# A conditioned block and two layers on one core: products of p @ w_ple moved to the ends of three projections, sums of squares added on VectorE

## The chip, the core and the metric

One core of one Trainium2 chip runs the whole program. The time is device microseconds of one execution. The engines are TensorE (PE; its weight loads are PEld), VectorE (DVE), ScalarE (ACT), GpSimd (POOL, nearly unused here) and SyncE (SP), which issues the loads. A line such as L357 is a line of the kernel.

## What is computed

256 tokens of width 2048 go through a block with conditioning (first_block) and two layers. What matters here:

```
# end of first_block's mixer, and what follows
x = x + gt_a * merge_heads(att_l, conv_l, g_mix_out, w_out)      # mix @ w_out
hf_l = modulate(rms_norm(x, g_ffn_norm), sh_f, sc_f)
x = x + gt_f * conv_ffn(hf_l, w_up, ffn_conv_w, ffn_conv_b, w_down)
x = rms_norm(x, g_final)
# the two layers i = 0, 1 (mixers A and B)
    h = mixer(x, ..., w_o)                      # (o * silu(gate)) @ w_o
    x = layer_norm(ALPHA * x + h, ln_g[i], ln_b[i])
    x = x + (p[i] @ w_ple[i]) * sigmoid(x @ w_ple_gate[i])
```

p[i] is an input of 256 x 256 and w_ple[i] is 256 x 2048, so p @ w_ple depends on nothing that the program computes.

## The kernel before

Activations lie with the features on the 128 partitions: X is [128, 16 tiles, 256 tokens]. Everything is float32, and each product is made of three: the weight is split into a high part wh (a cast on ScalarE, L357) and a low part wl (a subtraction on VectorE, L358), the activation into XH and XL in the same way, and TensorE adds wh·XH, wl·XH and wh·XL (L409). A unit is a piece of weights of 128x1024, 24 products of 256 columns.

The weights come from memory as raw chunks of 1 MB, two units each, through one queue on SyncE (L338), in a fixed order that plan() writes down. There are four raw buffers and five of split weights. unit() first splits up to four units ahead (look), unless hold() says that they must wait: units of w_up and w_pg are split ahead only for the first three, (0,0), (0,2) and (1,0) (group, first k tile). Between the units of the first block, chunks of w_ada ("late" events, L347, 128x2048 each) are summed on VectorE in the same order.

A projection of 2048 columns is computed in groups of 512 or 256 columns (_specs). MR and SR hand out accumulators in PSUM; a group's first product waits until the accumulator's last reader is done. Work that follows a group (gen) is written as generators that pump() takes a step further after each unit; this fixes every engine's order when the program is built. Each engine then runs its instructions strictly in that order.

resid(...) is a projection that ends in a residual sum: after each group upd adds its tiles to X; squares (sqr, on ScalarE) are added up in acc on VectorE; the last group's squares go one by one through a product with a matrix of ones (sums), which gives the sum over all features (s). It serves w_out (of the first block, groups 512, 512, 512, 256, 256), w_down, and the output projections woA and woB of the two layers (four groups of 512).

At the end of w_out, rstd makes the norm's factor RF, hf_first() the first two tiles of XH and XL for w_up, and hf(1) the next two. The layers' finish_layer issues the load of p (PF, "pf"), runs resid for the output projection with fin(0) converting PF to PH and PL, then the first group of w_ple, the sums, the second group, the norm's steps (gen_ln), the third and fourth groups, and then w_pg, whose first pairs of tiles are normed by pair(q). keep copies the ple products from PSUM to PW.

In the views in_wout, in_wada, in_woA, in_pt and so on are the inputs in memory, s and m accumulators in PSUM, rsm and RF the norm's numbers in the first block, mu, var and rsl those of a layer, and ADA the sums over w_ada.

Of the kernel before, what the change touches and what calls it, by code (L numbers as in the profile page):

```python
# [78 lines left out]
def _specs():  # L79
# [16 lines left out]
        "woA": (KD, [512] * 4),  # L96
# [6 lines left out]
        "woB": (KD, [512] * 4),  # L103
# [5 lines left out]
def _layout(kt, groups):  # L109

    chunks, cur, off = [], [], 0
    for g, w in enumerate(groups):
        uk = 1024 // w
        for k0 in range(0, kt, uk):
            nk = min(uk, kt - k0)
            if off + nk * w > 2048 or (kt > 2 and cur and cur[0][0] != g):
# [96 lines left out]
def _body(st, tc, A, out, dbg):  # L213
# [3 lines left out]
    lay = {n: _layout(*s) for n, s in spec.items()}  # L217
# [64 lines left out]
    plan_with_late("wout", [0, 4, 1, 5, 2, 6, 3, 7] + list(range(8, 16)))  # L282
    three = [4 * g + c for c in range(4) for g in range(3)]
    plan_with_late("wup", three + list(range(12, len(lay["wup"]))))
    for n in ("wdown", "wiq", "wik", "wka", "wva", "wqA", "wgA", "woA", "wple0", "wpg0", "wkb", "wvb", "wqB",
              "wgB", "woB", "wple1", "wpg1"):
        c = list(range(len(lay[n])))
        plan(n, three + c[12:] if n in ("wpg0", "wpg1") else c)
# [5 lines left out]
    pp = st.enter_context(tc.tile_pool(name="pp", bufs=1, space=PSUM))  # L294

# [120 lines left out]
    def unit_b(name, g, pst, xh, xl, starts=(0, 2)):  # L416

        u = unit(name, g)
# [102 lines left out]
    ones = cp.tile([P, P], F32, name="ones")  # L521
    identb = cp.tile([P, P], BF16, name="identb")
# [22 lines left out]
    def newton(dst, m):  # L545

        S.activation(dst, m, AF.Ln)
# [20 lines left out]
    with tc.tile_pool(name="b0", bufs=1) as b0:  # L568
# [29 lines left out]
        V.memset(ones, 1.0)  # L598

# [408 lines left out]
    def resid(pool, name, xh_, xl_, upd, acc, fin=None, pre=None, first=(), into=None):  # L1008
# [3 lines left out]
        n_acc = acc.shape[1]  # L1012
        tot = []

        def gen(g, m):
# [22 lines left out]
            if g == 2:  # L1038
                V.tensor_tensor(acc[:, :, 0], acc[:, :, 0], acc[:, :, 1], OP.add)
                for _ in range(3):  # L1040
                    yield
                b = yield from SR.get()
                mm(b.t[:, :n_acc * T], ones, acc[:, :, 0], True, False)
                tot.append(b)
# [4 lines left out]
        sq = pool.tile([P, 4, T], F32, name="sqe", tag="sqe")  # L1049

# [6 lines left out]
        def sums(ns):  # L1057
            for n in ns:
                if n_acc == 2:
                    mm(tot[0].t[:, T:], ones, X[:, n, :], False, n == 15)  # L1060
                mm(tot[0].t[:, :T], ones, sq[:, n - 12], False, n == 15)

        def gen_end(m, ns):
            yield
            end(m, ns)
            while not tot:
                yield
            for _ in range(3):
                yield
            sums(ns)  # L1070

        halves = len(spec[name][1]) == 5
        if halves:
            EV.add(gen_end(group_b(name, 3, xh_, xl_), (12, 13)))
            pump()
            end(group_b(name, 4, xh_, xl_), (14, 15))
        else:
            end(group_b(name, 3, xh_, xl_), range(12, 16))
# [5 lines left out]
        if fin:  # L1084
            fin(3)

# [4 lines left out]
        def finish():  # L1091
# [3 lines left out]
            sums((14, 15) if halves else range(12, 16))  # L1095
# [40 lines left out]
    with tc.tile_pool(name="b2", bufs=1) as b2:  # L1136
# [9 lines left out]
        b = resid(b2, "wout", xh, xl, upd_out, acc, first=m_out)()  # L1146
        rstd(RF, b.t[:, :T], 1.0 / D, EPS)
# [43 lines left out]
        hf_first()  # L1191
        for _ in hf(1):
            pass

        AC = b2.tile([P, NF, T], F32, name="AC")

# [58 lines left out]
        fin2 = resid(b2, "wdown", lambda k, u: u.x[:, 0, k - u.k0], lambda k, u: u.x[:, 1, k - u.k0], upd_down, acc, fin_lo, fin_hi, into=RF)  # L1255
        dump("x2", X)

        def gen_rf():
# [4 lines left out]
            yield from rstd_steps(RF, tot2.t[:, :T], 1.0 / D, EPS)  # L1263
# [69 lines left out]
    def finish_layer(pool, layer, wo, wp, wg, last):  # L1333

        PF = pool.tile([P, 2, T], F32, name="pf")
        nc.sync.dma_start(PF, A["pt"][layer])
        PH = pool.tile([P, 2, T], F32R, name="ph")
        PL = pool.tile([P, 2, T], F32R, name="pl")
        acc = pool.tile([P, 2, 2, T], F32, name="accl")
        PW = pool.tile([P, KD, T], F32, name="PW")  # L1340

# [3 lines left out]
        def fin(g):  # L1345
            if g == 0:
                pin()
                S.copy(PH, PF)
                V.tensor_tensor(PL, PF, PH.bitcast(F32), OP.subtract)

        finish = resid(pool, wo, xh, xl, upd, acc, fin)
# [4 lines left out]
        def gen_ln(tot):  # L1356
            ps = tot.t
            V.tensor_scalar(mu, ps[:, T:], 1.0 / D, None, op0=OP.mult)
            V.tensor_tensor(v, mu, mu, OP.mult)
            V.scalar_tensor_tensor(v, ps[:, :T], 1.0 / D, v, op0=OP.mult, op1=OP.subtract)  # L1360
            tot.free()
            V.tensor_scalar(v, v, 0.0, LN_EPS, op0=OP.max, op1=OP.add)
            yield from newton(rs, v)
            V.tensor_tensor(mu, mu, rs, OP.mult)
            both(pair(0), pair(1))
# [13 lines left out]
        def ple(g):  # L1379
            return group_b(wp, g, lambda k, u: PH[:, k, :], lambda k, u: PL[:, k, :])  # L1380

        def keep(g, m):
            S.copy(PW[:, 4 * g:4 * g + 4, :], four(m.t))
            m.free()

        m0 = ple(0)
        ln = gen_ln(finish())
        m1 = ple(1)
        keep(0, m0)
        next(ln)  # L1390
# [521 lines left out]
```

## Time and profile before

| | |
|---|---|
| three runs | 2202.58, 2196.92, 2197.62 us (median 2197.62) |
| profiled execution | 2194.55 us, span 2192.7 us |
| mean granted clock of TensorE | 0.993 |
| busy share of the span | TensorE 98%, VectorE 68%, ScalarE 50% |
| moved by DMA | 467.71 MB, mean 213 GB/s |
| chain that ended last | TensorE 94%, DMA 2%, VectorE 2%, ScalarE 1% |

The busy share says how long an engine had an instruction in hand. The chain is followed back from the last instruction, at each step to what released it. A row of a timeline has in brackets how long the engine stood idle before the instruction and which instruction ended that.

### The profile page before, as it was taken

How to read it: one execution, taken by the hardware profiler on the slowest of the kernel's cores; microseconds unless marked ns; L12 is line 12 of the kernel's file. 1: busy time of each engine (PE TensorE's matmuls, PEld its weight loads, DVE VectorE, ACT ScalarE, POOL GpSimd, SP SyncE). 2: the span in 40 equal slices, each digit the busy share in tenths (PEclk: the TensorE clock that was granted, in tenths of full speed). 3: DMA queues.
4: the chain of work that ended last, by engine and by line, in shares of the span. 5: the costliest groups of instructions: out<-in, count | busy, mean ns of one | idle time of the engine just before them, and what ended most of it. 6: DMA issues, size and time to landing. Idle time of an engine off the chain costs nothing.

```text
span 2192.7 us, 40082 instructions
## 1 busy us (share of the span) xinstructions
PE 2148.4 (98%) x17272; PEld 2058.8 (94%) x17272; DVE 1494.7 (68%) x1992; ACT 1104.9 (50%) x1512; POOL 0.2 (0%) x4
## 2 busy tenths in 40 slices
PE   5999999999999999999999999999999999999999
PEld 3779789989999999999999999999999999999999
DVE  4457878878767676757877669666666746646575
ACT  4345455445544444445656443445446546645363
POOL 0000000000000000000000000000000000000000
PEclk9999999999999999999999999999999999999999
DMA  9874878867666666645555544444555554455553
GB/s 395 335 278 175 324 260 308 344 242 288 230 223 239 231 233 236 223 176 190 187 187 187 186 164 177 150 154 154 197 174 181 188 192 142 147 173 190 181 176 113
DMA packets 68434, 467.71 MB, mean 213 GB/s; under 512 B 7840, under 2 KB 8352, under 8 KB 16544
## 3 DMA queue, kind: packets, MB, share of 16 engines
q1 hardware_dynamic: 68256, 465.14, 58.6%
q8 instruction: 135, 2.21, 0.4%
q14 instruction: 43, 0.35, 0.0%
HBM read 463.01 MB, written 2.10 MB: 212 GB/s over the span
## 4 chain that ended last, share of the span: by engine, by line
PE 94%; DMA 2%; DVE 2%; ACT 1%; issue 0%; SPq 0%; DVEq 0%; ACTq 0%
PE m L409 80%; PE s L409 14%; DMA raw<-in_wada 1%; DMA rawx<-in_wqa 1%; PE s L406 1%; DVE wl L358 1%; ACT wh L357 0%; DMA X<-in_xt 0%; DVE sq L616 0%; DVE raw L347 0%; DVE rp L1285 0%; DVE rp L1286 0%; DVE X L1144 0%; ACT uf L1204 0%; DVE uf L1212 0%
## 5 line engine op out<-in xcount | busy, mean ns | idle before, releaser
L409 PE MATMUL m<-XH,wh 128*128 128x256 f32 x4032 | 1144.8, 284 | 5.8 <-ACT XH L1185 4.1
L358 DVE TENSOR_TENSOR wl<-raw,wh 128x1024 fp32r<-128x1024 f32 (+1 forms) x672 | 800.2, 1197 | 502.9 <-ACT wh L357 501.6
L409 PE MATMUL m<-XH,wl 128*128 128x256 f32 x4032 | 1133.2, 281 | 2.9 <-DVE wl L358 2.9
L409 PE MATMUL m<-XL,wh 128*128 128x256 f32 x4032 | 1133.2, 281 | 0.3 <-DVE XL L1188 0.3
L357 ACT CAST wh<-raw 128x1024 fp32r<-128x1024 f32 (+1 forms) x672 | 687.0, 1029 | 665.8 <-PE m L409 587.4
L409 PEld LDWEIGHTS m<-XH,wh 128*128 128x128 f32 x4032 | 762.7, 189 | 27.6 <-issue 20.7
L409 PEld LDWEIGHTS m<-XH,wl 128*128 128x128 f32 x4032 | 762.5, 189 | 6.4 <-DVE wl L358 3.3
L409 PEld LDWEIGHTS m<-XL,wh 128*128 128x128 f32 x4032 | 762.2, 189 | 0.7 <-DVE XL L1188 0.6
L409 PE MATMUL m<-ahl,wh 128*128 128x256 f32 x1376 | 245.0, 281 | 0.5 <-DVE uf L1213 0.5
L409 PEld LDWEIGHTS m<-ahl,wh 128*128 128x128 f32 x1376 | 211.3, 188 | 0.7 <-issue 0.7
L409 PE MATMUL m<-ahl,wl 128*128 128x256 f32 x688 | 193.1, 281 | 0.0
L347 DVE SCALAR_TENSOR_TENSOR raw<-raw,CBC 128x2048 f32<-128x2048 f32 x64 | 145.0, 2283 | 0.0
L409 PEld LDWEIGHTS m<-ahl,wl 128*128 128x128 f32 x688 | 129.7, 189 | 0.0
L409 PE MATMUL s<-XH,wh 128*128 128x256 f32 x416 | 117.9, 283 | 7.1 <-ACT XH L649 7.1
L409 PE MATMUL s<-XL,wh 128*128 128x256 f32 x416 | 117.9, 283 | 0.0
L409 PE MATMUL s<-XH,wl 128*128 128x256 f32 x416 | 117.6, 283 | 0.0
L362 ACT CAST ahl<-AC 128x512 fp32r<-128x512 f32 x88 | 53.7, 610 | 89.0 <-PE m L409 89.0
L409 PEld LDWEIGHTS s<-XH,wh 128*128 128x128 f32 x416 | 79.4, 191 | 7.3 <-ACT XH L649 7.3
L363 DVE TENSOR_TENSOR ahl<-AC,ahl 128x512 fp32r<-128x512 f32 x88 | 59.6, 677 | 38.5 <-ACT ahl L362 38.5
L409 PEld LDWEIGHTS s<-XH,wl 128*128 128x128 f32 x416 | 79.4, 191 | 0.0
L409 PEld LDWEIGHTS s<-XL,wh 128*128 128x128 f32 x416 | 79.4, 191 | 0.0
L358 DVE TENSOR_TENSOR wl<-rawx,wh 128x768 fp32r<-128x768 f32 (+1 forms) x24 | 25.0, 1046 | 60.7 <-ACT wh L357 60.7
(387 smaller groups left out, 1683.4 us busy)
## 6 DMA issues: line engine op xcount, KB each, us to landing
raw<-in_wada SPq DMA_DIRECT2D x96, 1024.0 KB, 7.0
raw<-in_wup SPq DMA_DIRECT2D x86, 1024.0 KB, 4.9
raw<-in_wdown SPq DMA_DIRECT2D x40, 1024.0 KB, 4.8
raw<-in_wpg SPq DMA_DIRECT2D x32, 1024.0 KB, 4.9
raw<-in_wconv SPq DMA_DIRECT2D x28, 768.0 KB, 5.6
raw<-in_wout SPq DMA_DIRECT2D x16, 1024.0 KB, 6.4
raw<-in_wqA SPq DMA_DIRECT2D x16, 1024.0 KB, 4.8
raw<-in_wgA SPq DMA_DIRECT2D x16, 1024.0 KB, 4.8
```

Source lines behind the costliest of these rows:

```text
L347: V.scalar_tensor_tensor(r, r, 1.0, CBC, op0=OP.mult, op1=OP.mult, accum_out=ADA[:, b:b + 1])
L357: S.copy(e.wh[:, :n], r)
L358: V.tensor_tensor(e.wl[:, :n], r, e.wh[:, :n].bitcast(F32), OP.subtract)
L362: S.copy(e.x[:, 0, :e.nk], a)
L363: V.tensor_tensor(e.x[:, 1, :e.nk], a, e.x[:, 0, :e.nk].bitcast(F32), OP.subtract)
L406: count[0] = TE.transpose(o, i, ident)
L409: count[0] = TE.matmul(ps, l, r, start=start, stop=stop, skip_group_check=True, **kw)
```

## The change

It has five parts.

- The groups of p @ w_ple are computed elsewhere: layer 0's groups 0 and 1 at the end of w_out; layer 0's groups 2 and 3 and layer 1's group 0 at the end of woA; layer 1's groups 1 to 3 at the end of woB. The first of the three goes between a projection's last product and its sums. What a later layer needs is copied from PSUM by ScalarE (keep), stored in memory (plek) by a DMA that ScalarE issues, and loaded again by SyncE.
- p is loaded by parts(), which issues the DMA, the conversion on ScalarE and the subtraction on VectorE one after another, ahead of the projection's groups: in w_out for layer 0, in woA for layers 0 and 1 (both through one buffer pf), in woB for layer 1.
- woA and woB get groups of 512, 512, 512, 256, 256. In resid, squares and values of tiles 12 and 13 are added on VectorE; only the last two tiles go through ones on their own.
- ones holds 1/2048 from w_out on, so the sums are means; Ln reads PSUM directly (rstd_mean).
- The first two tiles of a layer's norm are handled one by one (first_pair), and w_pg's accumulators are handed out in another order.

```diff
-        "woA": (KD, [512] * 4),            # the same for woB
+        "woA": (KD, [512] * 3 + [256] * 2),
...
     plan_with_late("wout", [0, 4, 1, 5, 2, 6, 3, 7] + list(range(8, 16)))
+    plan("wple0", [0])
...
+        plan(n, three + c[12:] if n in ("wpg0", "wpg1") else c[1:] if n in ("wple0", "wple1") else c)
+        if n == "wple0":
+            plan("wple1", [0])
...
+    def rstd_mean(dst, src):
+        m = cp.tile([P, T], F32, name="rsm", tag="rsm")
+        S.activation(dst, src, AF.Ln, bias=eps[:, 0:1])
+        V.tensor_scalar(m, src, EPS, None, op0=OP.add)
+        yield from newton(dst, m, False)
...
+    def ple(layer, g, ph, ahead):
+        m = Banks(SR.now(), SR.now()) if ple_at[0] == 0 else MR.now()
+        ple_at[0] += 1
+        unit_b(f"wple{layer}", g, lambda n: m.bank(n // 2)[:, n % 2 * T:(n % 2 + 1) * T],
+               lambda k, u: ph[:, 0, k, :], lambda k, u: ph[:, 1, k, :], ahead=ahead)
+        return m
+
+    def keep(dst, m):
+        for b in range(2):
+            S.copy(dst[:, 2 * b:2 * b + 2, :], m.bank(b).rearrange("p (b t) -> p b t", b=2))
+        m.free()
+
+    def parts(pool, layer, tags):
+        pf = pool.tile([P, 2, T], F32, name="pf", tag=tags[0], bufs=tags[1])
+        ph = pool.tile([P, 2, 2, T], F32R, name="ph", tag=tags[2], bufs=tags[3])
+        nc.sync.dma_start(pf, A["pt"][layer])
+        S.copy(ph[:, 0], pf)
+        V.tensor_tensor(ph[:, 1], pf, ph[:, 0].bitcast(F32), OP.subtract)
+        return ph
...
+        def gen_end(m):                    # in resid: tiles 12 and 13
+            yield
+            end(m, (12, 13))
+            yield
+            V.tensor_tensor(acc[:, 0], acc[:, 0], sq[:, 0:2], OP.add)
+            if n_acc == 2:
+                V.tensor_tensor(acc[:, 1], acc[:, 1], X[:, 12:14, :], OP.add)
+            fold()
+            for _ in range(2):
+                yield
+            yield from total()
...
+        if fill:
+            fill()
...
-            sums((14, 15) if halves else range(12, 16))
+            if n_acc == 2:
+                mm(b.t[:, T:], ones, sq[:, 0], False, True)
+            for n in (14, 15):
+                mm(b.t[:, :T], ones, sq[:, n - 12], False, n == 15)
...
-        b = resid(b2, "wout", xh, xl, upd_out, acc, first=m_out)()
-        rstd(RF, b.t[:, :T], 1.0 / D, EPS)
+        V.memset(ones, 1.0 / D)
+        W4 = dict(tag="w4", bufs=4)
+        ph = parts(b2, 0, ("w4", 4, "w4", 4))
+        ple_out, ple_kept = [], dp.tile([P, 12, T], F32, name="plek")
+        def fill_out():
+            ple_at[0] = 0
+            ple_out.append(ple(0, 0, ph, 3))
+        b = resid(b2, "wout", xh, xl, upd_out, acc, first=m_out, fill=fill_out, sqe=W4)()
+        ple_out.append(ple(0, 1, ph, 2))
+        for _ in rstd_mean(RF, b.t[:, :T]):
+            pass
...
         hf_first()
-        for _ in hf(1):
-            pass
+        for g, m in enumerate(ple_out):
+            keep(AC[:, 4 * g:4 * g + 4, :], m)
+            nc.scalar.dma_start(ple_kept[:, 4 * g:4 * g + 4, :], AC[:, 4 * g:4 * g + 4, :])
+            if g == 0:
+                for _ in hf(1):
+                    pass
...
+        jobs = ((1, 1), (1, 2), (1, 3)) if last else ((0, 2), (0, 3), (1, 0))   # in finish_layer
+        ph = {}
+        for n in dict.fromkeys(l for l, _ in jobs):
+            ph[n] = parts(pool, n, ("pf", 1, f"ph{n}", 1))
+        if last:
+            nc.sync.dma_start(PW[:, 0:4, :], ple_kept[:, 8:12, :])
+        else:
+            nc.sync.dma_start(PW[:, 0:8, :], ple_kept[:, 0:8, :])
...
+        def fill(i=0):
+            n, g = jobs[i]
+            out_banks.append(ple(n, g, ph[n], 3 - i))
+        def store(i):
+            n, g = jobs[i]
+            if n == layer:
+                keep(PW[:, 4 * g:4 * g + 4, :], out_banks[i])
+            else:
+                t = pool.tile([P, 4, T], F32, name="pn")
+                keep(t, out_banks[i])
+                nc.scalar.dma_start(ple_kept[:, 8:12, :], t)
+        tot = resid(pool, wo, xh, xl, upd, acc, fin, fill=fill)()
+        fill(1)
+        fill(2)
+        # mu, var, rsl from tot on VectorE and ScalarE, store(0) and store(1) between
+        first_pair()
+        both(pair(1))
+        store(2)
```

VectorE around the third group of w_out. raw,ADA is a chunk of w_ada, wl a weight's low part, gta the gate's numbers, and X<-m,gta,X adds a group's four tiles to X and is the last reader of the group's accumulator. Before:

```order
L347 SCALAR_TENSOR_TENSOR raw,ADA<-raw,CBC 128x2048 x2
L358 TENSOR_TENSOR wl<-raw,wh 128x1024 x4
L1141 TENSOR_TENSOR gta<-ADA,vecs 128x16
L1144 SCALAR_TENSOR_TENSOR X<-m,gta,X 128x256 x4
L347 SCALAR_TENSOR_TENSOR raw,ADA<-raw,CBC 128x2048 x2
```

And after:

```order
L351 SCALAR_TENSOR_TENSOR raw,ADA<-raw,CBC 128x2048 x2
L362 TENSOR_TENSOR wl<-raw,wh 128x1024 x4
L1192 TENSOR_TENSOR gta<-ADA,vecs 128x16
L1197 MEMSET ones 128x128
L1041 TENSOR_TENSOR ph<-pf,ph 128x512
L1195 SCALAR_TENSOR_TENSOR X<-m,gta,X 128x256 x4
L351 SCALAR_TENSOR_TENSOR raw,ADA<-raw,CBC 128x2048 x2
```

The memset and the subtraction of p's parts now stand between gta and the four X operations.

ScalarE at the start of layer 0's output projection. GTA is the mixer's gate, XH<-OA the high part of the mixer's output. Before:

```order
L357 CAST wh<-raw 128x1024 x2
L1329 ACTIVATE GTA<-GTA 128x512
L563 CAST XH<-OA 128x512
L1329 ACTIVATE GTA<-GTA 128x512
L563 CAST XH<-OA 128x512
L357 CAST wh<-raw 128x1024 x10
L1027 ACTIVATE sqr<-X 128x512 x2
L357 CAST wh<-raw 128x1024
L555 ACT_TABLE_LOAD
L1348 CAST ph<-pf 128x512
```

And after:

```order
L361 CAST wh<-raw 128x1024 x2
L1396 ACTIVATE GTA<-GTA 128x512
L576 CAST XH<-OA 128x512
L1396 ACTIVATE GTA<-GTA 128x512
L576 CAST XH<-OA 128x512
L1040 CAST ph<-pf 128x512 x2
L361 CAST wh<-raw 128x1024 x10
L1077 ACTIVATE sqr<-X 128x512 x2
```

Two conversions of p, one for each layer, now stand ahead of the weight conversions that follow the mixer; before, one stood eleven weight conversions later.

ScalarE at the end of layer 0's output projection. sqe are the last squares, rsl and var the norm's numbers, PW and pn the ple products, wh the units of w_pg. Before:

```order
L1054 ACTIVATE sqe<-X 128x256 x4
L357 CAST wh<-raw 128x1024 x2
L1383 COPY PW<-m 128x1024
L547 ACTIVATE rsl<-var 128x256
L548 ACTIVATE rsl<-rsl 128x256
L1383 COPY PW<-m 128x1024
L1373 ACTIVATE X<-X,vecs 128x256 x2
L1375 CAST XH<-X 128x512
L1373 ACTIVATE X<-X,vecs 128x256 x2
L1375 CAST XH<-X 128x512
L357 CAST wh<-raw 128x1024
L1383 COPY PW<-m 128x1024 x2
```

And after:

```order
L361 CAST wh<-raw 128x1024 x3
L1100 ACTIVATE sqe<-X 128x256 x2
L560 ACTIVATE rsl<-var 128x256
L561 ACTIVATE rsl<-rsl 128x256
L1032 COPY PW<-s 128x512 x2
L1032 COPY PW<-m 128x512 x2
L1461 ACTIVATE XH<-X,vecs 128x256 x2
L1473 ACTIVATE X<-X,vecs 128x256 x2
L1475 CAST XH<-X 128x512
L1032 COPY pn<-m 128x512 x2
L1433 DMA plek<-pn 128x1024
L361 CAST wh<-raw 128x1024 x5
```

After the norm's numbers ScalarE now has four copies, the first two tiles, one pair, two copies and a DMA issue ahead of the next weight conversion.

## Rows read from the trace of the kernel before

**Rows 1.** The page: first the line of TensorE in the part on busy time (us, share of the span, instructions; the lines of the weight loads and of the other engines stand beside it), then the row of VectorE's sums over the chunks of w_ada among the costliest groups (busy us and mean ns of one, idle time before them).

```profile
PE 2148.4 (98%) x17272; PEld 2058.8 (94%) x17272; DVE 1494.7 (68%) x1992; ACT 1104.9 (50%) x1512; POOL 0.2 (0%) x4
...
L347 DVE SCALAR_TENSOR_TENSOR raw<-raw,CBC 128x2048 f32<-128x2048 f32 x64 | 145.0, 2283 | 0.0
```

**Rows 2.** The view by windows, core 0: start and end in us, length, then busy us and instructions of PE, PEld, DVE, ACT and POOL, the granted clock, the DMA engines' mean share and GB/s. The third group of w_out, the end of w_out (two rows), and a stretch inside w_up.

```profile
435.50:437.20 1.70, 0.25 (x3) 0.07 (x2) 1.70 (x5) 0.00 (x0) 0.00 (x0) 1.00 1.02 434
...
485.50:489.90 4.40, 0.30 (x3) 0.26 (x2) 2.96 (x10) 1.75 (x4) 0.00 (x0) 1.00 0.00 0
...
489.90:493.30 3.40, 3.08 (x14) 2.71 (x14) 1.91 (x5) 1.53 (x4) 0.00 (x0) 0.50 0.00 0
...
600.00:700.00 100.00, 100.00 (x854) 100.00 (x853) 68.45 (x81) 47.76 (x60) 0.00 (x0) 1.00 0.65 232
```

**Rows 3.** The chain that ended last, in order of time, at the third group of w_out: start us, us, what.

```profile
435.40 1.67 DVE X L1144 x4
...
437.21 2.85 PE m L409 x22
```

**Rows 4.** The timeline of SyncE, which issues the loads: start us, us, queue, line, transfer, count. Four places.

```profile
121.62 1.02 SPq L509 DMA_DIRECT2D cst<-in_cst  x2
...
435.31 0.33 SPq L338 DMA_DIRECT2D raw<-in_wout  x1
...
1545.88 0.33 SPq L1336 DMA_DIRECT2D pf<-in_pt  x1
...
1996.46 0.33 SPq L1336 DMA_DIRECT2D pf<-in_pt  x1
```

**Rows 5.** DMA issues by window (transfer, queue, count, KB, us from issue to landing): the chunk issued at 435.31, the wada chunk issued between 121.1 and 121.3, the transfer of constants issued at 121.62, and pf issued at 1545.88 and at 1996.46.

```profile
raw<-in_wout SPq DMA_DIRECT2D x1, 1024.0 KB, 6.6
...
raw<-in_wada SPq DMA_DIRECT2D x1, 1024.0 KB, 15.0
...
cst<-in_cst SPq DMA_DIRECT2D x1, 256.0 KB, 15.2
...
pf<-in_pt SPq DMA_DIRECT2D x1, 256.0 KB, 3.5
...
pf<-in_pt SPq DMA_DIRECT2D x1, 256.0 KB, 2.9
```

**Rows 6.** The instructions on tile pf (ns min/median/max, first and last start in us, form).

```profile
L1348 ACT CAST ph<-pf x2: 622/623/624, 1570.9 to 2021.6; 128x512 fp32r<-128x512 f32 x2
...
L1349 DVE TENSOR_TENSOR pl<-pf,ph x2: 686/686/687, 1572.7 to 2023.3; 128x512 fp32r<-128x512 f32 x2
```

**Rows 7.** The chain again, at the end of w_out.

```profile
485.57 0.44 DVE rsm L541
```

**Rows 8.** The timeline of TensorE at the end of w_out: start us, us, engine, line, operation, count, and in brackets the idle time before it and what ended it. The first row is the sums that follow w_out's last product, the second the first product of w_up.

```profile
483.22 1.02 PE L409 MATMUL s<-sqe,ones 128*128 128x256 f32 x4
...
489.64 0.38 PE L409 MATMUL m<-XH,wh 128*128 128x256 f32 x1 [4.10 <-ACT XH L1185]
```

**Rows 9.** The timelines of VectorE and ScalarE, as above: the second XL tile of w_up's first unit, the activations of hf(1), and a copy of 128x512 out of PSUM.

```profile
490.85 0.43 DVE L1188 TENSOR_TENSOR XL<-th,XH 128x256 fp32r<-128x256 f32 x1
...
491.92 1.09 ACT L1169 ACTIVATE th<-th,shf,G 128x256 f32<-128x256 f32 x2 [1.84 <-DVE th L1165]
...
1510.54 0.58 ACT L1511 COPY pa<-s 128x512 f32<-128x512 f32 x1
```

**Rows 10.** The timelines of ScalarE, VectorE and TensorE at the start of layer 0's output projection, and ScalarE at that of layer 1 (third row).

```profile
1545.04 2.94 ACT L357 CAST wh<-raw 128x1024 fp32r<-128x1024 f32 x3
...
1551.66 1.05 ACT L357 CAST wh<-raw 128x1024 fp32r<-128x1024 f32 x1 [1.76 <-PE m L409]
...
2002.06 1.05 ACT L357 CAST wh<-raw 128x1024 fp32r<-128x1024 f32 x1 [1.79 <-PE m L409]
...
1546.11 3.50 DVE L358 TENSOR_TENSOR wl<-raw,wh 128x1024 fp32r<-128x1024 f32 x3 [0.26 <-ACT wh L357]
...
1551.54 0.28 PE L409 MATMUL m<-XH,wl 128*128 128x256 f32 x1
```

**Rows 11.** The chain at the end of layer 0's output projection: sums, products with w_ple, first products of w_pg.

```profile
1634.10 3.45 PE s L409 x16
...
1637.55 8.48 PE m L409 x72
...
1646.03 5.70 PE s L409 x48
```

**Rows 12.** The timelines of VectorE and ScalarE in the same stretch: the mean, its square, the last step of the norm's numbers, the first step of pair 0, the activations of pairs.

```profile
1637.59 0.42 DVE L1358 TENSOR_SCALAR mu<-s 128x256 f32<-128x256 f32 x1 [1.07 <-PE s L409]
...
1638.05 0.42 DVE L1359 TENSOR_TENSOR var<-mu 128x256 f32<-128x256 f32 x1
...
1641.57 0.43 DVE L1364 TENSOR_TENSOR mu<-mu,rsl 128x256 f32<-128x256 f32 x1
...
1641.92 0.69 DVE L1369 TENSOR_TENSOR X<-X,rsl 128x512 f32<-128x512 f32 x1
...
1643.37 1.10 ACT L1373 ACTIVATE X<-X,vecs 128x256 f32<-128x256 f32 x2 [1.93 <-DVE X L1370]
```

**Rows 13.** The chain at the end of layer 1's output projection: sums, products with w_ple and the first of w_pg.

```profile
2085.50 3.45 PE s L409 x16
...
2097.58 5.63 PE s L409 x48
```

More of the change, by code (lines that the diff above doesn't have):

```diff
@@ L414, in mm3, with unit_b @@
         mm(ps, wh, xl, False, stop)
-    def unit_b(name, g, pst, xh, xl, starts=(0, 2)):
-        u = unit(name, g)
+    def unit_b(name, g, pst, xh, xl, starts=(0, 2), ahead=None):
+        u = unit(name, g, ahead)
         kt = spec[name][0]
@@ L1005, in _body, with resid, fold, total @@
         return
-    def resid(pool, name, xh_, xl_, upd, acc, fin=None, pre=None, first=(), into=None):
+    def ple(layer, g, ph, ahead):
[15 more added lines that the diff above has]
+        return ph
+    ple_at = [0]
+    def resid(pool, name, xh_, xl_, upd, acc, fin=None, pre=None, first=(), into=None, fill=None,
+              sqe=None):
         n_acc = acc.shape[1]
+        sqe = sqe or dict(tag="sqe")
         tot = []
+        halves = len(spec[name][1]) == 5
+        def fold():
+            V.tensor_tensor(acc[:, :, 0], acc[:, :, 0], acc[:, :, 1], OP.add)
+        def total():
+            b = yield from SR.get()
+            mm(b.t[:, :n_acc * T], ones, acc[:, :, 0], True, False)
+            tot.append(b)
         def gen(g, m):
@@ L1354, in finish_layer, with first_pair @@
         rs = pool.tile([P, T], F32, name="rsl")
[L1356 to L1365, printed above, removed]
+        ps = tot.t
+        V.tensor_copy(mu, ps[:, T:])
+        V.tensor_tensor(v, mu, mu, OP.mult)
+        V.tensor_tensor(v, ps[:, :T], v, OP.subtract)
+        V.tensor_scalar(v, v, 0.0, LN_EPS, op0=OP.max, op1=OP.add)
+        tot.free()
+        steps = newton(rs, v)
+        next(steps)
+        store(0)
+        next(steps, None)
+        V.tensor_tensor(mu, mu, rs, OP.mult)
+        store(1)
+        def first_pair():
+            for k in range(2):
+                x, g, b = X[:, k, :], vec(f"ln_g{layer}", k), vec(f"ln_b{layer}", k)
+                V.tensor_tensor(x, x, rs, OP.mult)
+                V.tensor_tensor(x, x, mu, OP.subtract)
+                S.activation(XH[:, k, :], x, AF.Identity, scale=g, bias=b)
+            for k in range(2):
+                x, g, b = X[:, k, :], vec(f"ln_g{layer}", k), vec(f"ln_b{layer}", k)
+                V.tensor_scalar(x, x, g, b, op0=OP.mult, op1=OP.add)
+                V.tensor_tensor(XL[:, k, :], x, XH[:, k, :].bitcast(F32), OP.subtract)
         def pair(q):
@@ L1377, in pair @@
             V.tensor_tensor(XL[:, ks, :], X[:, ks, :], XH[:, ks, :].bitcast(F32), OP.subtract)
[L1379 to L1390, printed above, removed]
-        keep(1, m1)
-        for _ in ln:
-            pass
-        m2, m3 = ple(2), ple(3)
-        keep(2, m2)
-        keep(3, m3)
+        first_pair()
+        both(pair(1))
+        store(2)
         def gen_ple(k0, nb, m):
```

67 lines of the change are left out of this document (27 added, 40 removed).

## The prediction

> **What bounds the kernel now.** I read the page first. TensorE is busy 98% of the span [rows 1], so a change is worth what it does to TensorE's stream and to the few places where that stream stands still. The windows give the stream's price: 854 products in 100 us, 0.117 us each [rows 2], so one unit of 24 products takes 2.81 us. They also show the two gaps that matter here. Before the third group of w_out TensorE did 0.25 us of work in 1.70 us and kept its full clock. At the end of w_out it did 0.30 us in 4.40 us, and the next 3.40 us ran at a granted clock of 0.50, which is 1.2 of 2.4 GHz [rows 2]. Those 3.40 us held 14 products, 1.64 us of work at full clock, so the lower clock cost 1.76 us.
>
> I name six places: P1 (third group of w_out, 435 us), P2 (end of w_out, 483), P3 and P5 (start of the output projections of layers 0 and 1, 1546 and 1996), P4 and P6 (their ends, 1631 and 2083). Elsewhere TensorE's products stay the same.
>
> **P1, parts() in w_out.** The chain says that TensorE's third group waits for VectorE's four X operations, which start at 435.40 and free its accumulator [rows 3]; ahead of them stands gta. In the new order of VectorE the subtraction of parts(), ph<-pf,ph, stands between gta and those X operations. It needs ScalarE's conversion of pf, and that needs the pf transfer, which SyncE issues right behind the 1 MB wout chunk of 435.31 [rows 4]. That chunk lands 6.6 us after its issue [rows 5], at 441.9. What a 256 KB transfer does behind such a chunk is shown by cst: issued at 121.62 behind a wada chunk issued between 121.1 and 121.3, it took 15.2 us where the chunk took 15.0 [rows 4, 5], so it landed some 0.65 us after it. I therefore put pf at 442.6. The conversion takes 0.62 us and the subtraction 0.69 us [rows 6]; with 0.03 us of issue the X operations start at 443.95 instead of 435.40: **+8.6 us**. Queued behind the two waits are ScalarE's weight conversions and VectorE's weight subtractions, but four units have been split ahead, 11 us of TensorE's work, so they hide. The lower bound is nothing, if pf were there before 435.4. The Trainium skill, "DMA: Bandwidth & Descriptors", section "Rules for kernel authors", advises to issue a transfer early and to wait on it late; parts() waits at once. By that advice, followed here, P1 and P3 would add nothing; the order of the instructions decides otherwise.
>
> **P2, products of p @ w_ple at the end of w_out.** T0 is 483.22, when the last w_out product is followed by the sums [rows 8]. Before, the sums end at 485.55, the first product of w_up starts at 489.64 and the second XL, which the unit's sixth product needs, is there at 491.28 [rows 7 to 9]. Counting back 16 products from 493.30, where the clock is full again, gives a start of 491.43 at full speed, T0 + 8.2. After: 24 products of the first ple group (2.81) and four sum records, eight before, at 0.216 each (3.45 for 16 [rows 11]) end at T0 + 3.7; from there the same chain runs, shorter by one VectorE operation (L541, 0.46 with its gap), so the second XL is there at 3.7 + 5.73 − 0.46 = 8.97 and w_up starts as if at 8.97 − 5 × 0.117 = 8.4. The second ple group (2.81) fits in the chain. Two stalls follow, because the copies AC<-s and AC<-m and two DMA issues (0.33 each, as on SyncE [rows 4]) come ahead of work on ScalarE. One copy of 128x512 out of PSUM takes 0.58 [rows 9]. hf(1)'s conversion: XH to 8.4, two copies 1.16, DMA 0.33, two activations 1.09 [rows 9], a cast 0.62, XL 0.69 ends at 12.3; TensorE wants it at 8.4 + 2.81 + 0.25 = 11.5, stall 0.8. Unit (1,0), no longer split ahead because the two ple units take two of five split buffers: VectorE has an ada chunk (2.28 [rows 1]) and then wl (1.2 [rows 10]) behind that XL, 15.8; wanted at 8.4 + 0.8 + 2 × 2.81 + 0.12 = 15.0, stall 0.8. Together T0 + 10.0: **+1.8 us**. The lower bound is the one without stalls, +0.2.
>
> **P3, layer 0's output projection.** Two pf transfers share one buffer. The first lands 3.5 us after 1545.88 [rows 4, 5], at 1549.4; with 0.62 and 0.69 its subtraction ends at 1550.75; only then is the second issued. I take 3.2 us, between 2.9 and 3.5 [rows 5]: 1554.0. ScalarE's second conversion ends at 1554.65, and behind it stand the conversion and subtraction of the fifth unit of woA (1.0 and 1.2 [rows 10]), done at 1556.9. Before, that conversion was the one of 1545.04, and TensorE took the unit's second product at 1551.54 [rows 10]. **+5.4 us**, 5.1 to 5.7. The 1 MB PW load behind them on SyncE is read only at P4 and costs nothing as long as raw chunks, taken at 0.65 of the DMA engines' time [rows 2], catch up.
>
> **P5.** One pf, 1996.46 + 2.9 [rows 5] + 0.62, then 1.05 and 1.2: the fifth unit is ready at 2002.3. At P3 TensorE's second product of that unit ran 0.12 us ahead of the next conversion on ScalarE (1551.66); the same conversion is at 2002.06 here [rows 10]: wanted at 2001.9. **+0.4 us**.
>
> **P4 and P6, ends of the projections.** Before, T0 is 1634.10 less 2.81 for the ple group in front, 1631.29, and w_pg starts at 1646.03 without a gap: 14.7 us, made of 96 ple products, 11.3, and 16 sum records, 3.45 [rows 11]. Of the 96, 24 are moved to P2 per layer; of the 16 records 6 stay (0.216 each). So the pure work after is 8.4 + 1.3 = 9.7: the change takes 5.0 us of work from TensorE here. But then the norm's chain is bare. After T0: ple 2.81, sums 1.3, at 4.1. The chain from the sums' end, 1637.55, to mu's product, 1642.00, takes 4.4 [rows 11, 12]: 8.5. The new first pair then does four 256-wide VectorE steps at 0.46 [rows 12], a scaling and XL for each tile: the second XL at 12.1, so w_pg starts as if at 11.5, and its first unit ends at 14.3. The second unit, (0,2), is not split ahead any more. ScalarE reaches its conversion after pair(1)'s two 512-wide VectorE steps (12.1 + 1.4), its activations and cast (1.1 + 0.6), the two pn copies (1.16) and a DMA issue (0.33): 16.7, then 1.05 and 1.2: 19.0 against a want at 14.4 [rows 6, 9, 12]. Start equivalent 11.5 + 4.6 = 16.1: **+1.3 us** at P4. At P6 there is no DMA and before it was 2097.58 − (2085.50 − 2.81) = 14.9 [rows 13], after 15.7: **+0.8 us**. If (0,2) isn't late, each is 3.3 to 3.5 us faster than before instead.
>
> **Clock.** P1 (10 us idle), P3 (5.4), P4 and P6 (4.6, 4.3) each leave TensorE idle as long as or longer than the 4.1 us at w_out's end [rows 8], which was followed by the half clock. I take 1.5 each, between 0 and 1.76: **+6.0 us**. At P2 the ple products fill the gap, so no fall is counted after.
>
> **Sum.** 8.6 + 1.8 + 5.4 + 1.3 + 0.4 + 0.8 = 18.3, with the clock 24.3. The profiled execution took 2194.55 us around a span of 2192.7; it lies 3.07 under the median of the three runs, 2197.62, and 2.4 under the lowest. 2194.55 + 24.3 = 2218.9; I forecast **2219 us**.
>
> **Rivals.**
> - *pf overtakes the megabyte at P1.* Its packets share 16 DMA engines with the chunk, whose windows are full there (share 1.02 [rows 2]). If it landed 2.9 to 3.5 us after issue, P1 would cost about 4.6 instead of 8.6: 2215. For it: pf alone takes that [rows 5]. Against it: cst behind the wada chunk. The Trainium skill, "DMA: Bandwidth & Descriptors", section "Queues, rings and completion order", says that each DMA engine takes descriptors of a ring in order but that whole transfers need not complete in the order of issue; cst agrees with the first half, and no row here shows the second. Chance 0.12.
> - *The casts of unit (0,2) are not late*, because ScalarE's copies wait less than I think or the unit is split ahead: P4 and P6 turn into −3.4 each and lose their clock fall, 8.9 + 3 less: 2207 to 2210. Chance 0.10.
> - *Not slower: the waits on pf are not met.* If ScalarE and VectorE reach parts() only after pf has landed, P1, P3 and P5 add nothing, and P2, P4 and P6 with their clock (3.9 + 3) leave +7, or less than that where a stall is short: 2198 to 2202, within 0.3% (6.6 us, about what this measurement can tell from no change). It decides where pf lands before 435.4 at P1, that is if SyncE issues it over 6 us earlier than the order shows. Chance 0.06. Both this and the former together would make it faster, 2190; chance 0.02.
>
> **How the numbers follow.** The main case, 0.70, has its own range, 2212 to 2226: the clock at nothing or at 1.76 four times, P2 without stalls, P3 at its ends. With the first rival and most of the second the range is 2207 to 2226. Slower by over 0.3%: 0.70 + 0.12 + 0.09 = 0.91 less what error of the whole sum may take, 0.89; same 0.08; faster 0.03.
>
> **What would show it.** P1: a gap of TensorE of about 10 us near 435 put down to X, and VectorE idle ahead of ph for over 6 us. P3: idle of about 5 us put down to a weight subtraction, with two pf transfers one behind the other. P2: no row of half clock at w_up's start. P4 and P6: 48 products behind the sums, then idle before w_pg's second unit. It is wrong if VectorE's wait for pf at 435 is under 3 us, or if (0,2) comes in time.

## The result and the profile after

The changed kernel takes 2230.78 us (median of four runs, 2228.43 to 2233.47) against 2197.27 us for the kernel before (four runs, 2196.76 to 2202.58): a ratio of 1.0149 with a 95% interval of 1.0135 to 1.0163. It is slower, as forecast, but by 33.5 us instead of the 21 to 24 of the forecast, and above the range's end of 2226.

The page of the changed kernel, its first line and the line of busy times:

```profile
span 2227.0 us, 40076 instructions
...
PE 2166.2 (97%) x17244; PEld 2073.3 (93%) x17248; DVE 1501.7 (67%) x2013; ACT 1106.5 (50%) x1520; POOL 0.2 (0%) x4
```

TensorE stays at 97% of a span that is 34.3 us longer (2192.7 before), and its busy time rose by 17.8 us ([rows 1]: 2148.4) although it has less to do (17248 weight loads instead of 17272). Products at half clock count as busy for longer, so this alone does not say where the time went, but it is the first sign of what the forecast lacks: about half of the loss is not idle time.

The waits of TensorE (engine, line, whom it waited for; us in total, times, the longest):

```profile
PE m L413 <- DVE X L1195: 9.9, 1, 9.9
...
PE m L413 <- ACT wh L361: 7.7, 3, 3.0
```

Before, TensorE did 0.25 us of work in the 1.70 us of the wait on X [rows 2], so it idled for 1.45; it is 9.9 now. Waits on wh did not stand among the larger ones before.

**P1.** The chain at the third group of w_out (start us, us, what):

```profile
433.44 6.89 DMA pf<-in_pt
...
440.36 0.63 ACT ph L1040
...
441.01 0.05 DVE ph L1041
...
441.62 1.66 DVE X L1195 x4
...
443.42 3.70 PE m L413 x18
```

It is the one that the forecast gives: pf's transfer, conversion, subtraction, then X, and only then TensorE. The DMA issues there (KB and us to landing):

```profile
raw<-in_wout SPq DMA_DIRECT2D x1, 1024.0 KB, 6.7
...
pf<-in_pt SPq DMA_DIRECT2D x1, 256.0 KB, 6.9
```

The chunk landed 6.7 us after 433.02, at 439.7, pf 6.9 us after 433.44, at 440.3: 0.6 us behind the megabyte, where 0.65 was worked out from [rows 4, 5].

**P2.** TensorE's timeline at the end of w_out: the sums, then the first products of w_up, with the idle time before them:

```profile
493.63 1.03 PE L413 MATMUL s<-sqe,ones 128*128 128x256 f32 x4
...
498.44 0.38 PE L413 MATMUL m<-XH,wh 128*128 128x256 f32 x1 [0.94 <-ACT XH L1247]
...
499.35 0.39 PE L413 MATMUL m<-XL,wh 128*128 128x256 f32 x1 [0.41 <-DVE XL L1250]
```

The 4.10 us gap of [rows 8] has become 0.94 and 0.41, filled by the ple products. The windows right after P1's and P2's gaps (the columns of [rows 2]):

```profile
443.40:446.40 3.00, 2.98 (x14) 3.00 (x15) 3.00 (x3) 0.53 (x1) 0.00 (x0) 0.50 0.00 0
...
501.10:504.30 3.20, 3.20 (x17) 3.20 (x16) 1.81 (x2) 2.77 (x6) 0.00 (x0) 0.50 0.30 119
```

The granted clock fell to 0.50 after both, and after P2 too, which the forecast had excluded: 17 products in 3.20 us.

**P3.** The chain at the start of layer 0's output projection:

```profile
1563.20 2.50 DMA pf<-in_pt
...
1565.78 0.63 ACT ph L1040
...
1566.43 0.70 DVE ph L1041
...
1567.15 2.60 DMA pf<-in_pt
...
1570.30 1.05 ACT wh L361
...
1571.38 1.24 DVE wl L362
...
1572.66 7.37 PE m L413 x47
```

The two transfers of pf stand one behind the other, 2.50 and 2.60 us, each with its conversion and subtraction. Only then come wh and wl of the fifth unit, and TensorE goes on at 1572.66.

**P4.** ScalarE at the end of that projection, from the activations of pair(1) to the conversion of w_pg's unit (0,2):

```profile
1668.00 1.09 ACT L1473 ACTIVATE X<-X,vecs 128x256 f32<-128x256 f32 x2 [2.30 <-DVE X L1470]
...
1669.65 1.06 ACT L1032 COPY pn<-m 128x512 f32<-128x512 f32 x2
...
1670.75 0.33 ACTq L1433 DMA_DIRECT2D plek<-pn  x1
...
1671.11 4.83 ACT L361 CAST wh<-raw 128x1024 fp32r<-128x1024 f32 x5 [0.40 <-ACT pn L1032]
```

and TensorE, whose next unit waits for that conversion and for wl:

```profile
1672.21 0.58 PE L413 MATMUL m<-XH,wh 128*128 128x256 f32 x1 [3.00 <-ACT wh L361]
...
1673.47 0.58 PE L413 MATMUL m<-XH,wl 128*128 128x256 f32 x1 [0.68 <-DVE wl L362]
```

The order is the forecast one: pair(1), the copies to pn, the DMA issue, then wh at 1671.11. Before, w_pg's first products ran without a gap [rows 11].

### The profile page after: what moved, and what is told of

Read it like the earlier page. It is cut to its first block, busy times and chain, and to the rows that moved or that the text cites. A ratio compares the mean times of both kernels' runs of the same rounds, so it can differ in the third digit from the quotient of the medians.

```text
span 2227.0 us, 40076 instructions
## 1 busy us (share of the span) xinstructions
PE 2166.2 (97%) x17244; PEld 2073.3 (93%) x17248; DVE 1501.7 (67%) x2013; ACT 1106.5 (50%) x1520; POOL 0.2 (0%) x4
## 4 chain that ended last, share of the span: by engine, by line
PE 90%; DVE 5%; DMA 3%; ACT 1%; issue 1%; SPq 0%; ACTq 0%; DVEq 0%
PE m L413 76%; PE s L413 13%; DMA raw<-in_wada 1%; DVE wl L362 1%; DMA rawx<-in_wqa 1%; PE s L410 1%; DMA pf<-in_pt 1%; DVE raw L351 0%; ACT wh L361 0%; DMA X<-in_xt 0%; DVE sq L630 0%; DVE rp L1352 0%; DVE rp L1353 0%; ACT X L1473 0%; DVE XL L1465 0%
```

## The experiments

### Is the extra time in the products themselves?

In a stretch of w_up without any wait the changed kernel does fewer products per 100 us (start and end, length, busy us and count of PE, ...):

```profile
600.00:700.00 100.00, 100.00 (x845) 100.00 (x844) 71.65 (x88) 46.59 (x56) 0.00 (x0) 1.00 0.66 234
```

845 against 854 of [rows 2], so 0.1183 us apart instead of 0.1171. (The expectations below give these spacings from the starts of neighbouring products, 0.1187 and 0.1173; the counts give the same step.) The products of this stretch were not changed. What did change is where their tiles lie: eps, a tile of 4 bytes allocated ahead of raw, wh and wl, takes 32 bytes, so they lie 32 bytes further up in SBUF (wh begins at byte 104832 of a partition instead of 104800), and with them everything that is allocated later. XH and XL lie ahead of eps and stay.

**before_pad32**: the kernel before, with eps and its memset alone.

```diff
     ones = cp.tile([P, P], F32, name="ones")
+    eps = cp.tile([P, 1], F32, name="eps")
...
         V.memset(ones, 1.0)
+        V.memset(eps, EPS)
```

> The kernel before with nothing but the new 4-byte tile eps and its memset, as the change allocates it: raw chunks, wh and wl then lie 32 bytes further up in SBUF. In the traces the products of w_up are 0.1173 us apart before and 0.1187 us after the change, with no stall between them. Theory A (the spacing follows where the tiles lie): about 12 us slower than before, 2209 us, with products 0.1187 apart in w_up. Theory B (the spacing has another cause, or differs between executions): within 3 us of before, 2197 us.

Measured: 2208.28 us (2206.45 to 2209.67), ratio 1.0046 [1.0031, 1.0061]. The same window:

```profile
600.00:700.00 100.00, 100.00 (x845) 100.00 (x844) 67.68 (x80) 46.91 (x58) 0.00 (x0) 1.00 0.67 231
```

845 again. Theory A holds: 11.5 us against the kernel before measured with it (2196.74), a third of the change's loss, come from the place of a four-byte tile and not from the work that was moved.

Not every stretch pays. A stretch of w_down without waits, in the kernel before and in before_pad32:

```profile
1000.00:1100.00 100.00, 100.00 (x845) 100.00 (x844) 74.80 (x102) 61.28 (x86) 0.00 (x0) 1.00 0.53 190
...
1000.00:1100.00 100.00, 100.00 (x845) 100.00 (x844) 76.88 (x105) 62.03 (x87) 0.00 (x0) 1.00 0.55 195
```

845 in both. VectorE's instructions of the two profiled executions, taken one by one, fall 5.5 us apart from the start of w_up to its end, 0.9 us in w_down and 6.7 us in pieces behind it.

**after_pad64**: the changed kernel with a larger eps.

```diff
-    eps = cp.tile([P, 1], F32, name="eps")
+    eps = cp.tile([P, 16], F32, name="eps")
```

> The changed kernel with eps made 64 bytes wide, so that every later tile moves by another 32 bytes: 64 in all against before. Theory A in its form 'alignment to 64 bytes': the spacing of before comes back, about 12 us less than the change, 2219 us. Theory A in its form 'any move' or theory B: no change, 2231 us within 3.

Measured: 2243.85 us (2240.35 to 2246.24), ratio 1.0204 [1.0183, 1.0224], slower by another 13 us; neither form of the expectation foresaw it. The window of w_up holds 835 products, 0.1198 us apart. So it is not a matter of 64-byte alignment.

**before_pad96, before_pad160, before_pad256**: the kernel before with eps of 96, 160 and 256 bytes (`[P, 24]`, `[P, 40]`, `[P, 64]`), a single execution each.

> The kernel before with a tile of 96 bytes where the change has eps: raw, wh and wl 96 bytes further up. With 0 bytes w_up's products stood 0.1173 us apart, with 32 bytes 0.1187, with 64 (in the changed kernel) 0.1200. If each 32 bytes add one step: 0.1213 in w_up, about 2232 us. If the spacing repeats every 64 or 128 bytes: 0.1187 or 0.1173 again, 2208 or 2197 us.

> The same with 160 bytes, which puts raw, wh and wl on multiples of 512 bytes (wh at 104960). If alignment to 512 bytes is what TensorE's weight reads want, the closest spacing of all, 0.1173 or less, 2197 us or less; if the spacing grows with the distance moved, 0.1200 or more, 2220 us or more.

> The same with 256 bytes: every address has the same remainder by 256 as in the kernel before. If the spacing follows the remainder by 256 or a part of it, it is that of before, 0.1173 in w_up, and 2197 us; if not, it follows the place itself or a larger remainder.

Measured: 2197.16, 2215.69 and 2193.17 us, with 851, 836 and 854 products in the window of w_up. Neither the alignment to 512 bytes nor a growth with the distance; 256 bytes bring back what 0 bytes gave.

**after_pad256**: the changed kernel with eps of 256 bytes (`[P, 64]`).

> The changed kernel with eps 256 bytes wide, so that every later tile keeps the remainder by 256 that it has in the kernel before. The 12 us that 32 bytes cost the kernel before should fall away and the waits stay: about 2219 us, products in w_up 0.1173 apart. If the spacing in the changed kernel has a second cause: 2225 us or more.

Measured: 2218.12 us (2216.22 to 2225.92), ratio 1.0104 [1.0081, 1.0128], 854 products in the window. With the tiles at the old remainders the changed kernel takes what the prediction's sum gave, 2219 us. Part of that match is luck: the sum put its 24.3 us on an execution that lay 3 us under the median. Against the kernel before measured with it (2198.13) the loss is 20.0 us, 17.8 to 28.1 by the interval.

### Do the waits cost what the gaps show?

**late**: the loads of p stay where they are, conversion and subtraction move behind the first group's sums (and the second pf's load behind the first conversion).

```diff
-        S.copy(ph[:, 0], pf)
-        V.tensor_tensor(ph[:, 1], pf, ph[:, 0].bitcast(F32), OP.subtract)
-        return ph
+        def convert():
+            S.copy(ph[:, 0], pf)
+            V.tensor_tensor(ph[:, 1], pf, ph[:, 0].bitcast(F32), OP.subtract)
+        return ph, convert
...
+        def fin_out(g):                    # handed to resid for w_out
+            if g == 0:
+                convert()
...
             if g == 0:                     # fin of finish_layer
                 pin()
+            if g < 2 and convert:
+                convert.pop()()
+                if todo:
+                    load()
```

> The changed kernel with the loads of p issued where they are, but the conversion and subtraction moved behind the first group's sums (the second pf of layer 0 behind the second group's). If the waits on pf cost what the gaps show, P1 gives back 8.5 us and 1.4 of half clock, P3 3.5 and 1.8: about 15 us less than the change, 2216 us. Rival: w_out is limited by its loads there, so that a stall of several us returns a few units later: 5 to 9 us less, 2222 to 2226 us.

Measured: 2215.61 us (2213.99 to 2220.03), ratio 1.0083 [1.0066, 1.0101]: 15.2 us less than the change. TensorE at P1 (timeline) and the chain at P3:

```profile
435.32 0.36 PE L413 MATMUL m<-XH,wh 128*128 128x256 f32 x1 [1.43 <-DVE X L1198]
```

```profile
1554.95 25.08 PE m L413 x209
```

The wait at P1 is back at 1.43 us; at P3 the chain is TensorE's own products through the whole stretch. Nothing came back later, so the rival falls.

**ahead**: one more unit split ahead at the second and third ple group of each place, w_out's end (P2) among them.

```diff
-        ple_out.append(ple(0, 1, ph, 2))
+        ple_out.append(ple(0, 1, ph, 3))
...
-            out_banks.append(ple(n, g, ph[n], 3 - i))
+            out_banks.append(ple(n, g, ph[n], (3, 3, 2)[i]))
```

> The changed kernel with three units instead of two split ahead at the second ple group (and two instead of one at the third), so that w_pg's unit (0,2) is converted before the norm's chain begins. If the stall before that unit is the cost, P4 gives back 4.3 us and 2.6 of half clock, P6 3.8 and 1.8: about 12 us less than the change, 2219 us. Rival: the conversion delays the norm's chain by as much as it saves at the unit: within 3 us of the change, 2231 us.

Measured: 2220.63 us (2215.97 to 2221.28), ratio 1.0098 [1.0082, 1.0115]: 10.2 us less than the change. ScalarE at P4, and the window of w_pg's second unit:

```profile
1657.93 1.03 ACT L361 CAST wh<-raw 128x1024 fp32r<-128x1024 f32 x1
...
1663.49 0.42 ACT L560 ACTIVATE rsl<-var 128x256 f32<-128x256 f32 x1 [4.52 <-DVE var L1446]
```

```profile
1672.00:1678.00 6.00, 5.27 (x40) 4.90 (x41) 3.78 (x4) 5.32 (x7) 0.00 (x0) 1.00 0.22 87
```

The conversion of (0,2) runs at 1657.93, between the last squares and the norm's logarithm, for which ScalarE would have waited anyway. The stretch in which the changed kernel stood 3.00 and 0.68 us and then ran at half clock keeps its full clock.

**both**: late and ahead together.

> The changed kernel with the edits of the kernels late and ahead together (eps 4 bytes wide, as in the change). They act at different places, so their gains over the change, 15.2 and 10.2 us, should add: 2205 to 2206 us. Rival: with P3's wait gone or P4's unit early, the work moves the next wait up, and less than 20 us are given back: 2211 us or more.

Measured: 2205.62 us (2204.05 to 2212.30), ratio 1.0055 [1.0035, 1.0076]. The gains add, 25.2 us of 25.3, as far as can be told: the runs come from different rounds and chips, between which the kernel before itself moved by up to 4 us (medians 2194.14 to 2198.13).

**both_pad256**: the same with eps of 256 bytes.

> The kernel both (conversions of p later, one more unit split ahead) with eps 256 bytes wide. Theory: both's 2205.6 less the 11.5 to 12 us of the moved tiles, 2194 us, against 2194 to 2197 of the kernel before: within 0.3% of it, if anything below. Rival: what is left of the change (later splits, copies and stores in w_out) is worth more than its saved sums and costs: above 2200 us.

Measured: 2195.71 us (12 runs, 2190.14 to 2201.49) against 2198.13 of the kernel before (16 runs): ratio 0.9990 [0.9977, 1.0003]. Without its waits and at the old remainders the change can't be told from no change.

### Which place gives which spacing?

**before_front32**: eps ahead of X, so that X, XH and XL move along.

> The kernel before with 32 bytes ahead of X, so that X, XH and XL move along with raw, wh and wl. If the spacing follows where the weights lie, 0.1187 in w_up as with 32 bytes behind XL, about 2208 us. If it follows where the weights lie against the activations that they meet, 0.1173 as before, 2195 to 2197 us.

Measured: 2211.26 us in a single execution, 835 products in the window of w_up. Neither: 845 was the count with the weights alone moved, 854 with nothing moved. So the place of the tiles ahead of eps, the activations' among them, counts as well, and not only as a distance to the weights'.

**both_pad224, both_pad192**: both with eps of 224 and 192 bytes.

> The kernel both with eps 224 bytes wide (remainder 64 of wh and wl by 256). Spacings in w_up so far: remainder 96: 0.1173, 128: 0.1187, 160: 0.1200, 192: 0.1178, 0: 0.1200. No theory says what 64 gives; between 0.1173 and 0.1200 the time is 2194 to 2219 us, and under 0.1173 it would be below the kernel before.

> The kernel both with eps 192 bytes wide (remainder 32 of wh and wl). The remainder between 0 and 64 that is missing: remainders 64 and 96 gave 0.1133 and 0.1173 in w_up, 0 gave 0.1200. If the spacing falls towards 64 from both sides: 0.115 to 0.118, 2165 to 2200 us.

Measured: 2159.51 us with 885 products in the window, and 2198.33 us with 848. With remainder 64 the products stand 0.1130 us apart, the closest of all, and the next steps on either side are as slow as before; it doesn't fall towards 64 from below.

**both_pad224_timed, before_pad224**: the first of these timed, and the kernel before with the same 224 bytes.

> The kernel both with eps 224 bytes wide, timed: 2159.5 us in one look, with 0.1133 in w_up. If that spacing belongs to the layout it is there in every execution: 2157 to 2164 us. If it was a state of that one execution: 2195 us in most.

> The kernel before with 224 bytes where the change has eps (remainder 64 of wh and wl by 256). If the place of the weights alone sets the spacing, as in both with 224 bytes: 0.1133 in w_up and about 2162 us. If the low spacing comes only with the change's order of work: 0.1173 or more and 2195 us or more.

Measured: 2162.11 us (2152.72 to 2174.30), ratio 0.9853 [0.9811, 0.9895], and 2157.82 us (2155.96 to 2174.60), ratio 0.9856 [0.9812, 0.9899]. before_pad224 in w_up and in w_down:

```profile
600.00:700.00 100.00, 100.00 (x885) 100.00 (x884) 75.53 (x92) 47.37 (x58) 0.00 (x0) 1.00 0.69 241
...
1000.00:1100.00 100.00, 100.00 (x854) 100.00 (x854) 79.55 (x112) 63.63 (x93) 0.00 (x0) 1.00 0.53 185
```

A pad of 224 bytes alone takes 38 us off the kernel before, more than the 33.5 us that the change with all its parts added. The change's order of work adds nothing to it that can be measured.

**both_front224**: both with 224 bytes ahead of raw, wh and wl, and 32 more behind wl, so that what lies after them has the old remainders.

```diff
         e.wl = rp.tile([P, 1024], F32R, name="wl", tag="wl", bufs=NSPL)
+        if not behind:
+            behind.append(rp.tile([P, 8], F32, name="behind"))
+            V.memset(behind[0], 0.0)
```

> The kernel both with 224 bytes ahead of raw, wh and wl and 32 more behind wl, so that in w_down the activations' parts ahl have remainder 0 again (224 before) while the weights keep 64. Spacing in w_down with 224 bytes alone: 0.1187. If it follows weights against activations, as in w_up, 0.1133 there, about 11 us less: 2149 us. If w_down has a spacing of its own: 2160 us.

Measured: 2160.02 us (2139.64 to 2163.11), ratio 0.9821 [0.9773, 0.9868]. In w_up and w_down:

```profile
600.00:700.00 100.00, 100.00 (x885) 100.00 (x884) 74.75 (x92) 47.84 (x58) 0.00 (x0) 1.00 0.69 243
...
1000.00:1100.00 100.00, 100.00 (x851) 100.00 (x851) 79.10 (x112) 63.76 (x92) 0.00 (x0) 1.00 0.53 186
```

851 in w_down, not 885: w_down has a spacing of its own at the same remainders. In w_up the count stays at 885 with everything behind wl back at its old remainder, so what a move of the tiles behind eps changes there is due to those from eps to wl, and of these w_up's products read wh and wl alone.

The four times spread over 23 us. That the addresses alone do not fix the spacing everywhere is seen in both_pad224 and both_pad224_timed, which are the same program. The same stretch of w_pg of layer 0, without any wait, in the first and in the second:

```profile
1660.00:1710.00 50.00, 50.00 (x444) 50.00 (x443) 37.17 (x41) 28.41 (x33) 0.00 (x0) 1.00 0.56 199
...
1660.00:1710.00 50.00, 50.00 (x427) 50.00 (x426) 34.82 (x37) 28.44 (x33) 0.00 (x0) 1.00 0.54 190
```

444 products in 50 us against 427. These two executions were on two chips, so which of the two, the execution or the chip, makes the difference is not shown by them; the four times of both_front224 are from one chip. In w_up no trace shows that: the kernels with the tiles moved by 0 or 256 bytes have 854 or 855 in all four traces, by 32 bytes 845 or 846 in all five, by 224 bytes 884 or 885 in all four.

The places tried, by the bytes that raw, wh and wl were moved:

| bytes | remainder of wh and wl by 256 | products per 100 us of w_up | us of the kernel before | us of the change, or of both |
|---|---|---|---|---|
| 0 | 96 | 854 | 2197.27 | - |
| 32 | 128 | 845 | 2208.28 | 2230.78; both 2205.62 |
| 64 | 160 | 835 | - | 2243.85 |
| 96 | 192 | 851 | 2197.16 | - |
| 160 | 0 | 836 | 2215.69 | - |
| 192 | 32 | 848 | - | both 2198.33 |
| 224 | 64 | 885 | 2157.82 | both 2162.11 |
| 256 | 96 | 854 | 2193.17 | 2218.12; both 2195.71 |

The times for 96, 160 and 192 bytes, and 2193.17, are single executions.

## Why the prediction was right and wrong, point by point

The direction was right, the time outside the range. The step that failed is the sentence "Elsewhere TensorE's products stay the same." Their number does; their spacing rose by 1.1% in w_up (854 to 845 per 100 us) and in other stretches, though not in w_down, and the sum has no term for it. The runs put that term at 11.5 us (before_pad32 alone; 6.8 to 13.4 by its interval), and without it the changed kernel takes 2218.12 us (after_pad256), inside the range. The diff has eps in it; that four bytes move every tile of weights was not looked at.

The rest can be checked against before_pad32, which has the new places and none of the work. Six instructions that both kernels have, in before_pad32 (timelines of VectorE and ScalarE: before P1, between P1 and P2, in w_up, at the third sums of woA, in layer 1, and the end):

```profile
427.03 2.29 DVE L347 SCALAR_TENSOR_TENSOR raw<-raw,CBC 128x2048 f32<-128x2048 f32 x1
...
466.31 2.29 DVE L347 SCALAR_TENSOR_TENSOR raw<-raw,CBC 128x2048 f32<-128x2048 f32 x1
...
621.95 0.68 DVE L1222 TENSOR_TENSOR AC<-uf 128x512 f32<-128x512 f32 x1
...
1621.96 1.15 ACT L1029 ACTIVATE sqr<-X 128x512 f32<-128x512 f32 x2
...
1845.76 1.22 DVE L1700 SCALAR_TENSOR_TENSOR QB<-m,QB 128x1024 fp32r<-128x1024 f32 x1
...
2202.56 0.69 DVE L1407 TENSOR_TENSOR sgl<-sgl,PW 128x512 f32<-128x512 f32 x1 [9.97 <-ACT sgl L1404]
```

and in the changed kernel:

```profile
423.78 2.29 DVE L351 SCALAR_TENSOR_TENSOR raw<-raw,CBC 128x2048 f32<-128x2048 f32 x1
...
472.88 2.28 DVE L351 SCALAR_TENSOR_TENSOR raw<-raw,CBC 128x2048 f32<-128x2048 f32 x1
...
630.74 0.69 DVE L1287 TENSOR_TENSOR AC<-uf 128x512 f32<-128x512 f32 x1
...
1635.13 1.15 ACT L1077 ACTIVATE sqr<-X 128x512 f32<-128x512 f32 x2
...
1863.74 1.22 DVE L1783 SCALAR_TENSOR_TENSOR QB<-m,QB 128x1024 fp32r<-128x1024 f32 x1
...
2222.56 0.69 DVE L1490 TENSOR_TENSOR sgl<-sgl,PW 128x512 f32<-128x512 f32 x1 [9.97 <-ACT sgl L1487]
```

The differences are −3.3, +6.6, +8.8, +13.2, +18.0 and +20.0 us. The −3.3 is there before any changed instruction. The places are compared in one execution of each kernel, so differences of some tenths of a us mean nothing. So:

| place | forecast, with the clock | measured |
|---|---|---|
| P1 | 8.6 + 1.5 = 10.1 | 9.8 |
| P2 | 1.8 | 2.2 |
| P3 | 5.4 + 1.5 = 6.9 | 4.4 |
| P4 and P5 | 1.3 + 1.5 + 0.4 = 3.2 | 4.8 |
| P6 | 0.8 + 1.5 = 2.3 | 2.0 |
| sum | 24.3 | 23.3 |

- **P1** holds in every step: the landing 0.6 us behind the megabyte, the two conversions, the half clock after it. That pf would overtake the chunk, as the first rival had it, did not happen. The measured 0.6 also agrees with the part of the Trainium skill's section "Queues, rings and completion order" ("DMA: Bandwidth & Descriptors") by which a ring's descriptors are taken in order.
- **P2** has the right size from two wrong halves, and that is luck. The two stalls of 0.8 hardly show (no wait there is over 0.4 us after the second XL), and the clock did fall: 17 products in 3.20 us, 2.0 us of work at 0.1183 each, so 1.2 us lost. The fall does not follow from the gaps alone. The kernel late has the same ones, and the window behind them shows the full clock:

```profile
489.01 0.39 PE L413 MATMUL m<-XH,wh 128*128 128x256 f32 x1 [0.97 <-ACT XH L1255]
...
489.92 0.39 PE L413 MATMUL m<-XL,wh 128*128 128x256 f32 x1 [0.41 <-DVE XL L1258]
```

```profile
491.70:494.90 3.20, 2.98 (x24) 2.70 (x24) 1.83 (x2) 2.77 (x6) 0.00 (x0) 1.00 0.31 122
```

  Of the eleven traces with these gaps (0.90 to 1.05 and some 0.41 us) seven keep the clock and four lose it, with P1's wait or without it. In late the two stalls do show, as 0.23 and 0.36 us.
- **P3**'s mechanism holds and its size was taken too high: pf landed 2.50 and 2.60 us after issue, under both rows that stood for it (2.9 and 3.5), and the fifth unit's second product came 3.5 us late instead of 5.4 (1572.66 for 1569.1).
- **P4** is larger than forecast, by the clock: the idle time was 3.00 and 0.68 us against 4.6, but the half clock after it lasted longer than the 3.40 us of [rows 2] (in late, after the same idle time, it did not). The window from P4's idle time on:

```profile
1672.40:1678.60 6.20, 5.52 (x25) 5.22 (x26) 6.17 (x7) 3.97 (x5) 0.00 (x0) 0.50 0.74 276
```

  25 products in 6.20 us are 3.0 us of work. **P5** adds nothing that can be seen, **P6** what was forecast. The landmarks for P4 take in some of the difference in spacing that is left between these two executions.
- The rival of unit (0,2) falls for the changed kernel, and the run ahead shows that its cause was rightly named: it is late only because it is not split ahead.
- The rival "not slower" falls with P1's chain. Its price was nearly right: late, which stands for that case, has P2, P4 and P6 left; it is 18.9 us above the kernel before measured with it (2196.74), and less the 11.5 us of before_pad32 some 7.3 remain, where the rival had 7 or less.

What stays open: why the place of the weights sets the spacing. The runs show that a move by 256 bytes leaves it as it was, that the tiles ahead of eps have a part in it (one execution), that w_down has another spacing than w_up at the same remainders, and that one program can run a stretch at two spacings. No run here separates wh from wl, or the products' reading of weights from their reading of activations.

both_front224 and before_pad224 are both faster than the kernel before; the second is the plain one, a single tile of 224 bytes.

## What to carry to other kernels

Before an edit's cost is summed up, compare the places of the tiles that TensorE reads, before and after: a tile of a few bytes ahead of them can change the spacing of the products in whole stretches, and a kernel bound by TensorE pays for it there. When a change is timed, time its layout alone beside it, and give small constants a place behind the large tiles. A conversion that waits for a load belongs where its engine gets to it after the landing, since everything behind it in the engine's order waits too.

## What the runs showed of the hardware that was not expected

- Products of 256 columns without any wait stood 0.1130 to 0.1198 us apart in w_up at full granted clock (885 to 835 per 100 us), by the place of raw, wh and wl in steps of 32 bytes: a range of 6% in w_up, and of 2157.82 to 2215.69 us, under 3%, in the kernel before as a whole.
- Moving them by 256 bytes gave the same count as not at all, 854.
- Kernels with the closest spacing vary more from run to run: 2139.64 to 2163.11 us, 2152.72 to 2174.30 and 2155.96 to 2174.60 in four runs each, where the kernel before kept within 2190.99 to 2199.51 in seven runs on the same chip.
- One program ran the same stretch of w_pg at 444 and at 427 products per 50 us in two executions, on two chips, both at full granted clock.
- The granted clock fell to 0.50 at w_up's start though TensorE had idled for only 0.94 and 0.41 us there; in late it stayed at 1.00 after idle times of 0.97 and 0.41.
